# Sample's self-attention in units of a head and 256 queries, with background work dealt out per unit

## The chip, the cores and the metric

The kernel runs on one core of a Trainium2 chip. The metric is the device time of one execution, in microseconds (us). The engines are named as in the profile: PE is TensorE (matmuls; PEld are its weight loads), DVE is VectorE, ACT is ScalarE, POOL is GpSimd, SP is SyncE, which here issues every DMA, in order, from one queue.

## The reference

One layer of an encoder is applied to two groups of requests with the same weights: prompt (1024 tokens) and sample (512 tokens). Everything is in float32. What matters here:

```python
z = rms_norm(x, ln_pre) @ w_in          # q, k, v, gates, merge logits, pool and cross inputs
s = einsum('bqkgd,bskd->bkgqs', qblk, k) * HEAD_DIM ** -0.5   # 8 heads, 2 kv heads, head size 64
p = softmax(s)                          # over all 1024 (prompt) or 512 (sample) keys
attn_out = einsum('bkgqs,bskd->bqkgd', p, v)
cross_out = softmax(xq @ mk.T * XHD ** -0.5) @ mv             # 4 heads, 256 memory tokens
branches = pool_out * silu(g0), attn_out * silu(g1), cross_out * silu(g2)
merged = sum over n of sigmoid(merge_logits_n + b_n) * (branches[n] @ w_branch[n])
y = x + rms_norm(merged @ w_out, ln_post)
```

## The kernel before

Float32 products are made of float32r parts: a value is split in a high part (a copy on ACT) and a low part (a subtraction on DVE), `split` (L171), and a product takes three matmuls, or two where one side holds both parts side by side.

The projections of prompt come first, then those of sample that its attention needs. What is left of sample's projections (32 output tiles of 24 matmuls each: gates and merge logits) is the *fill*: `weave` (L108) emits it a half tile (12 matmuls) at a time between the steps of a *stream* of attention units, so that PE has work while the softmax of a unit runs on the other engines. When the stream is through, what is left of the fill is emitted, and then the branch projections of prompt (`branches(0, sc, merged)`, L1039), which load the prompt's branch outputs `br0`, `br2` and `br1` from DRAM.

The stream is (L1034 to L1037): prompt's self-attention (64 units), prompt's cross-attention (8), sample's self-attention (32), sample's cross-attention (4). A unit of self-attention is a head and 128 queries. It has four steps:

- `ahead`: the load of q, two units early.
- `scores`: matmuls of q with the keys into a PSUM tile `A` of 128x1024, the maximum (DVE), the exponential (ACT) with its sum read out, the reciprocal (DVE), the normalisation (POOL).
- `turn`, two units later: the transposes of the probabilities into a second `A` tile, and their split into `med` tiles.
- `values`, two more units later: the products with v into a PSUM tile `B`; then, for every pair of units, a copy of one half (L810, ACT), a sum (L811, DVE), and for every pair of heads the gating (L813, POOL) and the store to `br1` (L814).

There are two `A` buffers, and scores and transposes take them in turn, so the next unit's scores wait until the exponential of this unit has been read out. With 1024 keys a unit of prompt fills an `A` tile. With 512 keys a unit of sample fills half of it: two score matmuls, four transposes and four value matmuls, and a maximum, exponential, split on 512 columns.

`weave` adds up the PE cost of each step (a 512-column matmul counts 213 ns, a transpose 107 ns), times 0.66 (`SHARE`), and emits fill until that much is paid. A step that emits no matmuls earns no fill: in the first iterations of the stream there are scores alone.

The order on each engine is then decided by a scheduler, in which `high_priority` moves instructions ahead: the evacuations of PSUM by 200 (`EVAC`), the maximum and exponential by 150 (`PMAX`), the split of transposes by 150 (`PTURN`). The SP queue holds stores and loads in one order, and a store that waits for its data holds up the loads behind it.

## Time and profile before

| | |
|---|---|
| median of 3 runs | 1512.16 us (1507.26 to 1512.44) |
| profiled execution | 1511.38 us, span 1509.6 us |
| PE busy | 1462.9 us, 97% of the span |
| DVE, ACT, POOL busy | 981.2, 709.2, 272.4 us |
| the stream of attention units | from 695 to 1171.5 us of the span |
| sample's self-attention in it | from about 1047 to 1143 us |

PE is the engine that the span is made of; a microsecond is won or lost where PE stands still or runs at its lower clock. Rows of a timeline merge instructions of one kind that follow each other: start, length, engine, line, operation, tiles, and in brackets the time for which the engine sat idle before, with what ended it. A matmul's length holds its latency; what a matmul costs in a row of them is the distance of their starts.

### The profile page before, as it was taken

The numbers are of one execution on the slowest core, as the hardware profiler recorded it, in microseconds if no ns is written. First come the engines' busy times: TensorE is split into PE (matmuls) and PEld (weight loads), VectorE is DVE, ScalarE is ACT, GpSimd is POOL, SyncE is SP. The second block draws the span as 40 slices with busy tenths as digits, with TensorE's granted clock in tenths as the row PEclk, the third lists the DMA queues.
The fourth block names the chain that finished last, engine by engine and source line by source line (L and its number), as shares of the span: only waits on it lengthen the run. The fifth ranks groups of instructions, "written<-read, shape, count | busy, mean of one in ns | idle before, by whom it ended". The sixth has DMA issues, their size and how long they took to land.

```text
span 1509.6 us, 19658 instructions
## 1 busy us (share of the span) xinstructions
PE 1462.9 (97%) x7264; PEld 1207.9 (80%) x7264; DVE 981.2 (65%) x1262; ACT 709.2 (47%) x1097; POOL 272.4 (18%) x286
## 2 busy tenths in 40 slices
PE   5999999999999999999999999999989999999998
PEld 3778888888888888887888888888767878888887
DVE  5896586666648564646676676666667664764754
ACT  5354444544434544434565555666666323323332
POOL 0001020110000000301222222233233150150241
PEclk8999999999999999999999999999999999999999
DMA  7333234332323433344322222265326854954952
GB/s 274 100 112 110 84 112 126 106 132 65 127 91 93 155 119 126 112 138 138 91 65 78 96 65 90 81 213 185 126 72 233 313 179 138 338 192 141 337 163 84
DMA packets 88174, 211.37 MB, mean 140 GB/s; under 512 B 9872, under 2 KB 19216, under 8 KB 87312
## 3 DMA queue, kind: packets, MB, share of 16 engines
q1 hardware_dynamic: 88080, 210.14, 42.1%
q8 instruction: 57, 0.93, 0.3%
q14 instruction: 37, 0.30, 0.1%
HBM read 155.57 MB, written 54.53 MB: 139 GB/s over the span
## 4 chain that ended last, share of the span: by engine, by line
PE 83%; issue 4%; ACT 4%; DVE 4%; DMA 2%; POOL 1%; SPq 0%; DVEq 0%; POOLq 0%; ACTq 0%
PE B L133 65%; PE A L133 13%; PE A L137 5%; ACT u L769 1%; DMA hu<-xq 1%; DVE wlo L169 1%; ACT med L172 1%; ACT whi L172 1%; DVE s L767 1%; PE B L137 1%; DMA hu<-merge 1%; POOL med L925 1%; POOL s L196 0%; DVE med L169 0%; DMA med<-q 0%
## 5 line engine op out<-in xcount | busy, mean ns | idle before, releaser
L133 PE MATMUL B<-med,whi 128*128 128x512 f32 x2776 | 870.3, 393 | 1.1 <-ACT hu L359 1.1
L133 PEld LDWEIGHTS B<-med,whi 128*128 128x128 f32 x2776 | 513.5, 188 | 104.5 <-ACT hu L359 2.3
L133 PE MATMUL B<-med,wlo 128*128 128x512 f32 x1388 | 542.6, 391 | 0.7 <-DVE wlo L169 0.7
L172 ACT ACTIVATE whi<-raw 128x1024 fp32r<-128x1024 f32 (+1 forms) x168 | 167.3, 996 | 304.4 <-PE B L133 212.6
L133 PEld LDWEIGHTS B<-med,wlo 128*128 128x128 f32 x1388 | 260.7, 188 | 55.9 <-DVE wlo L169 1.7
L169 DVE TENSOR_TENSOR wlo<-raw,whi 128x1024 fp32r<-128x1024 f32 (+1 forms) x168 | 213.0, 1268 | 139.3 <-ACT whi L172 136.8
L172 ACT ACTIVATE med<-A 128x1024 fp32r<-128x1024 f32 (+1 forms) x108 | 96.9, 897 | 121.3 <-PE A L137 121.1
L771 POOL TENSOR_SCALAR u<-u,s 128x1024 f32<-128x1024 f32 (+1 forms) x96 | 94.6, 985 | 317.0 <-DVE s L770 275.7
L169 DVE TENSOR_TENSOR med<-A,med 128x1024 fp32r<-128x1024 f32 (+1 forms) x109 | 115.7, 1061 | 51.6 <-ACT med L172 50.0
L767 DVE TENSOR_REDUCE s<-A 128x1 f32<-128x1024 f32 (+1 forms) x96 | 100.1, 1043 | 42.7 <-PE A L133 20.8
L192 POOL TENSOR_SCALAR s<-s 128x16 f32<-128x16 f32 (+3 forms) x17 | 6.6, 388 | 671.8 <-DVE s L557 324.6
L769 ACT ACTIVATE u<-A,s 128x1024 f32<-128x1024 f32 (+1 forms) x96 | 93.1, 970 | 46.3 <-DVE s L767 45.8
L137 PE MATMUL A<-ident,u 128*128 128x128 f32 x784 | 107.2, 275 | 4.6 <-DVE med L169 2.1
L137 PEld LDWEIGHTS A<-ident,u 128*128 128x128 f32 x784 | 90.8, 141 | 24.8 <-issue 9.6
L133 PE MATMUL A<-kt,med 128*128 128x512 f32 x320 | 96.5, 415 | 10.0 <-ACT u L769 8.8
L925 POOL TENSOR_TENSOR med<-med,hu 128x512 f32<-128x512 f32 x48 | 77.4, 1625 | 136.1 <-DVE hu L923 136.1
L133 PE MATMUL A<-whi,med 128*128 128x512 f32 (+1 forms) x320 | 92.4, 368 | 0.2 <-ACT hu L954 0.2
L172 ACT ACTIVATE whi<-sum 128x1024 fp32r<-128x1024 f32 x50 | 53.1, 1062 | 64.3 <-PE B L133 62.1
L133 PEld LDWEIGHTS A<-kt,med 128*128 128x128 f32 x320 | 54.4, 190 | 34.2 <-ACT u L769 22.9
L133 PE MATMUL B<-med,vt 128*128 128x256 f32 x512 | 76.1, 288 | 1.4 <-ACT med L172 1.4
L169 DVE TENSOR_TENSOR med<-med,med 128x1024 fp32r<-128x1024 f32 (+1 forms) x50 | 55.5, 1115 | 33.7 <-ACT med L172 29.9
L172 ACT ACTIVATE med<-med 128x1024 fp32r<-128x1024 f32 (+1 forms) x44 | 44.3, 1019 | 68.8 <-POOL med L925 42.6
(173 smaller groups left out, 1567.2 us busy)
## 6 DMA issues: line engine op xcount, KB each, us to landing
raw<-wt SPq DMA_DIRECT2D x168, 512.0 KB, 3.7
merge<-hu SPq DMA_DIRECT2D x72, 256.0 KB, 2.1
hu<-merge SPq DMA_DIRECT2D x72, 256.0 KB, 5.4
med<-br SPq DMA_DIRECT2D x36, 256.0 KB, 5.2
q<-hu SPq DMA_DIRECT2D x24, 256.0 KB, 2.6
br<-hu SPq DMA_DIRECT2D x24, 256.0 KB, 2.5
med<-q SPq DMA_DIRECT2D x12, 512.0 KB, 4.5
med<-xt_prompt SPq DMA_DIRECT2D x4, 1024.0 KB, 13.2
```

The costliest lines, as they stand in the source:

```text
L133: pe.matmul(out, l, r, **k)
L137: pe.transpose(out, x, i[:])
L169: v.tensor_tensor(out, x, hi.bitcast(F32), op=ALU.subtract)
L172: act.activation(hi, x, AF.Copy)
L192: pool.tensor_scalar(ss, ss, EPS, 1.0, op0=ALU.add, op1=ALU.mult)
L767: v.reduce_max(mx[:], a[:, :L], axis=AX.X, negate=True)
L769: act.activation(p[:, :L], a[:, :L], AF.Exp, bias=mx[:], accum_out=sm[:])
L771: pool.tensor_scalar(p[:, :L], p[:, :L], rc[:], 1.0, op0=ALU.mult, op1=ALU.mult)
L925: pool.tensor_tensor(at, at, sg[:], op=ALU.add)
```

## The change

Sample's attention gets a function of its own, `pairs_of`, with units of a head and 256 queries (16 units). The two query tiles of a unit share one `A` tile: four score matmuls, one maximum over both, two exponentials (each with its own maximum and its own sum), one reciprocal, two normalisations, eight transposes into one `A` tile, one split of 1024 columns, eight value matmuls. The count of matmuls, transposes and exponentials of the whole kernel stays the same. The end of a unit (L803 to L814) moves into `gated`, which both kinds of attention call.

`weave` no longer measures a step's cost. Each unit carries a number (2560 for self-attention, 3410 for cross-attention), and each iteration of the stream yields a third of it, times `SHARE`, three times: after scores, turn and values, whether or not such a step exists in that iteration. So the first iterations earn as much fill as the later ones, and so do the last four, in which the units run out.

```diff
-    def weave(main, fill, share):
+    def weave(main, fill):
         owed = 0.0
-        for _ in with_cost(main):
-            owed += _ * share
+        for more in main:
+            owed += more
             while owed > 0:
                 c = cost[0]
                 if next(fill, fill) is fill:
...
+    def pairs_of(sc, kt, vt):
+        qd, gd, out = sc["q"], sc["attn_gate"], sc["br1"]
+        units = [(jp, hd) for jp in range(TT // 2) for hd in range(NH)]
...
+        def scores(i):
+            jp, hd = units[i]
+            g = hd // (NH // NG)
+            a, p = A(), U()
+            mx, sm, rc = S(2), S(2), S(2)
+            for j in range(2):
+                q, ns = state["q", jp][:, j * D + hd * P:j * D + (hd + 1) * P], slice(j * BLK, (j + 1) * BLK)
+                mm(a[:, ns], q, kt[g][0], start=True, stop=False)
+                mm(a[:, ns], q, kt[g][1], start=False, stop=True)
+            with tc.high_priority(PMAX):
+                v.reduce_max(mx[:], a[:].rearrange("p (j n) -> p j n", j=2), axis=AX.X, negate=True)
+                for j in range(2):
+                    ns = slice(j * BLK, (j + 1) * BLK)
+                    act.activation(p[:, ns], a[:, ns], AF.Exp, bias=mx[:, j:j + 1], accum_out=sm[:, j:j + 1])
+            v.reciprocal(rc[:], sm[:])
+            for j in range(2):
+                ns = slice(j * BLK, (j + 1) * BLK)
+                pool.tensor_scalar(p[:, ns], p[:, ns], rc[:, j:j + 1], 1.0, op0=ALU.mult, op1=ALU.mult)
+            state[i] = p
+
+        def turn(i):
+            p, tp, pt = state[i], A(), M()
+            for c in range(4):
+                for j in range(2):
+                    tr(tp[:, c * 256 + j * P:c * 256 + (j + 1) * P], p[:, j * BLK + c * P:j * BLK + (c + 1) * P], ident)
+            with tc.high_priority(PTURN):
+                split(pt[:, :D], pt[:, D:], tp[:])
+            state[i] = pt
...
+        return [(ahead, scores, turn, values, i, 2560) for i in range(len(units))]
...
     def stream(units):
         n = len(units)
         for i in range(-2, n + LAG + VLAG):
+            more = units[min(max(i, 0), n - 1)][5] * SHARE / 3
             for k, lag in enumerate((-2, 0, LAG, LAG + VLAG)):
                 if 0 <= i - lag < n:
                     units[i - lag][k](units[i - lag][4])
-                    yield
+                if k > 0 and i >= 0:
+                    yield more
...
-    units += attention(0, scs, kts, vts, 512) + cross(0, scs, mkd[0], mvd[0])
-    weave(stream(units), fill, SHARE)
+    units += pairs_of(scs, kts, vts) + cross(0, scs, mkd[0], mvd[0])
+    weave(stream(units), fill)
```

What this does to the order is shown at three places. In the rows after the change the line numbers are those of the changed kernel: L126 and L130 are the matmul and the transpose, L139 the load, L165 the copy of a split. The first is PE at the start of the stream, in the kernel before: the transposes of the first unit (`A<-ident` x8), three matmuls of a pool projection, the scores of the fourth unit (`A<-kt`), the transposes of the second unit, and the first value matmul (`B<-med,vt`).

```order
L137 MATMUL A_5482<-ident,u_5431 128x128 x8
L133 MATMUL B_5523<-med_5330,hu_5317 128x512 x3
L133 MATMUL A_5493<-kt_651,med_5419 128x512
L133 MATMUL A_5493<-kt_652,med_5419 128x512
L133 MATMUL A_5493<-kt_651,med_5419 128x512
L133 MATMUL A_5493<-kt_652,med_5419 128x512
L137 MATMUL A_5530<-ident,u_5463 128x128 x8
L133 MATMUL B_5567<-med_5480,vt_655 128x256
```

The same place on PE after the change (`B<-med,whi` and `B<-med,wlo` are fill):

```order
L130 MATMUL A_5506<-ident,u_5431 128x128 x8
L126 MATMUL B_5547<-med_4493,whi_5543 128x512 x2
L126 MATMUL B_5547<-med_4493,wlo_5544 128x512
L126 MATMUL B_5547<-med_4493,whi_5543 128x512 x2
L126 MATMUL B_5547<-med_4493,wlo_5544 128x512
L126 MATMUL B_5547<-med_4496,whi_5543 128x512 x2
L126 MATMUL B_5547<-med_4496,wlo_5544 128x512
L126 MATMUL B_5547<-med_4496,whi_5543 128x512 x2
L126 MATMUL B_5547<-med_4496,wlo_5544 128x512
L126 MATMUL A_5517<-kt_651,med_5419 128x512
```

Twelve matmuls of fill now stand between the first transposes and the fourth unit's scores, where three pool matmuls stood; those three, and two of fill, now stand between the second unit's transposes and the first value matmul.

The second place is ACT in the middle of sample's self-attention. Before, each unit has one split of its transposes (`med<-A`, L172) and one exponential (`u,s<-A`, L769); in between stand copies of value halves (L810), a tanh of the fill (L480) and the split of the fill's next weights (`whi<-raw`):

```order
L172 ACTIVATE med_9375<-A_9399 128x4x128
L769 ACTIVATE u_9395,s_9392<-A_9388,s_9391 128x512
L172 ACTIVATE med_9429<-A_9430 128x4x128
L480 ACTIVATE hu_9449<-B_9343,hbias 128x512
L769 ACTIVATE u_9425,s_9422<-A_9418,s_9421 128x512
L810 ACTIVATE hu_9410<-B_9452 64x256
L172 ACTIVATE whi_9721<-raw_9719 128x1024
L769 ACTIVATE u_9464,s_9461<-A_9457,s_9460 128x512
L172 ACTIVATE med_9429<-A_9468 128x4x128
```

After (L165 is the split, L825 the exponential, L860 the copy, L473 the tanh), three units in a row:

```order
L860 ACTIVATE hu_9322<-B_9354 64x256
L825 ACTIVATE u_9328,s_9330<-A_9327,s_9329 128x512 x2
L165 ACTIVATE med_9402<-A_9401 128x1024
L825 ACTIVATE u_9387,s_9389<-A_9386,s_9388 128x512
L860 ACTIVATE hu_9422<-B_9413 64x256
L825 ACTIVATE u_9387,s_9389<-A_9386,s_9388 128x512
L165 ACTIVATE med_9443<-A_9442 128x1024
L825 ACTIVATE u_9428,s_9430<-A_9427,s_9429 128x512
L473 ACTIVATE hu_9466<-B_9373,hbias 128x512
L860 ACTIVATE hu_9422<-B_9469 64x256
L825 ACTIVATE u_9428,s_9430<-A_9427,s_9429 128x512
L165 ACTIVATE whi_9680<-raw_9678 128x1024
```

The split now stands ahead of the unit's two exponentials, and in two units of three a copy, or a tanh and a copy, stands between the two. On PE the three units read: scores, 8 transposes, 5 value matmuls, 12 of fill; scores, 8 transposes, 8 value matmuls, 7 of fill; scores, 8 transposes, 5 of fill, 11 value matmuls.

The third place is the end of the stream, on PE and on SP. Before, on PE: the values of the last two heads of sample's cross-attention (`B<-med,med` x6 each), a last half tile of fill, and then the first branch matmul of prompt (`med_10328`, the split of `br0`):

```order
L133 MATMUL B_10286<-med_10230,med_9931 128x512 x6
L133 MATMUL B_10297<-med_10253,med_9931 128x512 x6
L133 MATMUL B_10273<-med_4499,whi_10269 128x512 x2
L133 MATMUL B_10273<-med_4499,wlo_10270 128x512
L133 MATMUL B_10273<-med_4499,whi_10269 128x512 x2
L133 MATMUL B_10273<-med_4499,wlo_10270 128x512
L133 MATMUL B_10273<-med_4502,whi_10269 128x512 x2
L133 MATMUL B_10273<-med_4502,wlo_10270 128x512
L133 MATMUL B_10273<-med_4502,whi_10269 128x512 x2
L133 MATMUL B_10273<-med_4502,wlo_10270 128x512
L133 MATMUL B_10344<-med_10328,whi_10338 128x512 x2
```

After, on PE (`med_10168` is the split of `br0`):

```order
L130 MATMUL A_10095<-ident,u_9973 128x128 x8
L126 MATMUL B_10107<-med_9992,med_9704 128x512 x6
L130 MATMUL A_10118<-ident,u_10026 128x128 x8
L126 MATMUL B_10130<-med_10064,med_9704 128x512 x6
L126 MATMUL B_10141<-med_10104,med_9704 128x512 x6
L126 MATMUL B_10152<-med_10127,med_9704 128x512 x6
L126 MATMUL B_10184<-med_10168,whi_10178 128x512
```

The fill is used up before the last two transposes, and the first branch matmul stands right behind the last value matmul. On SP before (`br_0_c` are the stores of sample's cross-attention heads, `med<-br_1_c` the four loads of prompt's `br0`):

```order
L814 DMA br_0_3_4512<-hu_10091 128x256
L885 DMA br_0_0_4513<-hu_10240 128x512
L146 DMA raw_10450<-wt 128x1024
L146 DMA med_10323<-br_1_0_595 128x512
L146 DMA med_10323<-br_1_1_596 128x512
L885 DMA br_0_1_4514<-hu_10263 128x512
L146 DMA med_10323<-br_1_2_597 128x512
L146 DMA med_10323<-br_1_3_598 128x512
L885 DMA br_0_2_4515<-hu_10293 128x512
L146 DMA u_11121<-x_prompt 128x1024
L885 DMA br_0_3_4516<-hu_10304 128x512
```

On SP after:

```order
L474 DMA merge_1_7_4544<-hu_10092 128x512
L139 DMA hu_10137<-x_gate_1_4522 128x512
L139 DMA hu_10148<-x_gate_2_4523 128x512
L139 DMA hu_10159<-x_gate_3_4524 128x512
L936 DMA br_0_0_4513<-hu_10114 128x512
L139 DMA med_10163<-br_1_0_595 128x512
L936 DMA br_0_1_4514<-hu_10137 128x512
L936 DMA br_0_2_4515<-hu_10148 128x512
L139 DMA med_10163<-br_1_1_596 128x512
L936 DMA br_0_3_4516<-hu_10159 128x512
L139 DMA med_10163<-br_1_2_597 128x512
L139 DMA med_10163<-br_1_3_598 128x512
```

The second load of `br0` now stands behind the third of the four stores, and the last two loads behind the fourth; before, all four stood ahead of the third.

## Rows read from the trace of the kernel before

**Rows 1.** Busy time by stretch: from:to, us, each engine, PE's clock, DMA.
```profile
704.00:716.00 12.00, 9.29 (x39) 7.44 (x40) 6.48 (x9) 4.64 (x8) 2.24 (x2) 0.72 0.34 99
...
750.00:1000.00 250.00, 246.74 (x1459) 207.53 (x1457) 167.65 (x207) 149.53 (x220) 67.21 (x64) 1.00 0.29 92
1047.00:1143.00 96.00, 88.84 (x498) 70.30 (x497) 65.68 (x122) 58.98 (x125) 29.43 (x40) 1.00 0.41 135
1143.00:1171.50 28.50, 27.46 (x162) 23.03 (x161) 19.92 (x27) 18.70 (x48) 9.32 (x18) 1.00 0.60 195
```

**Rows 2.** Timeline of PE at the start of the stream, fourth to sixth unit.
```profile
705.53 1.21 PE L133 MATMUL A<-kt,med 128*128 128x512 f32 x4 [1.84 <-ACT u L769]
...
706.81 1.84 PE L137 MATMUL A<-ident,u 128*128 128x128 f32 x8
...
709.76 0.58 PE L133 MATMUL B<-med,vt 128*128 128x256 f32 x1 [1.11 <-ACT med L172]
```

**Rows 3.** PE's groups from 1047 to 1143 us, shapes apart.
```profile
L133 PE MATMUL B<-med,whi 128*128 128x512 f32 x98 | 33.8, 403 | 0.0
L133 PE MATMUL A<-kt,med 128*128 128x512 f32 x64 | 22.2, 428 | 5.1 <-ACT u L769 5.0
L133 PE MATMUL B<-med,med 128*128 128x256 f32 x116 | 20.3, 293 | 0.2 <-ACT med L172 0.2
L137 PE MATMUL A<-ident,u 128*128 128x128 f32 x136 | 20.2, 273 | 1.8 <-DVE med L169 1.5 <-ACT u L769 0.2
L133 PE MATMUL B<-med,wlo 128*128 128x512 f32 x48 | 19.1, 397 | 0.0
L133 PE MATMUL B<-med,med 128*128 128x512 f32 x24 | 6.4, 402 | 0.0
L133 PE MATMUL A<-med,u 128*128 128x256 f32 x12 | 1.7, 292 | 0.0
```

**Rows 4.** Timeline of one prompt unit, from scores to the next scores.
```profile
764.70 1.08 PE L133 MATMUL A<-kt,med 128*128 128x512 f32 x4
...
765.61 1.03 PE L137 MATMUL A<-ident,u 128*128 128x128 f32 x8
...
766.40 1.19 PE L133 MATMUL B<-med,vt 128*128 128x256 f32 x8
766.68 1.02 ACT L172 ACTIVATE med<-A 128x1024 fp32r<-128x1024 f32 x1 [2.35 <-PE A L137]
767.43 0.64 PE L133 MATMUL B<-med,whi 128*128 128x512 f32 x2
767.60 1.11 ACT L769 ACTIVATE u<-A,s 128x1024 f32<-128x1024 f32 x1
...
768.83 0.38 ACT L810 ACTIVATE hu<-B 64x256 f32<-64x256 f32 x1
768.86 1.19 PE L133 MATMUL A<-kt,med 128*128 128x512 f32 x4
```

**Rows 5.** Timeline of ACT in sample's self-attention.
```profile
1074.90 0.68 ACT L769 ACTIVATE u<-A,s 128x512 f32<-128x512 f32 x1
...
1075.56 0.69 ACT L480 ACTIVATE hu<-B,hbias 128x512 f32<-128x512 f32 x1
1076.13 1.06 ACT L172 ACTIVATE whi<-raw 128x1024 fp32r<-128x1024 f32 x1
```

**Rows 6.** Timeline of the stream's end.
```profile
1166.05 2.88 PE L133 MATMUL B<-med,med 128*128 128x512 f32 x12
1166.20 0.93 SPq L146 DMA_DIRECT2D med<-br  x2
...
1167.61 0.69 DVE L884 TENSOR_TENSOR hu<-B,hu 128x512 f32<-128x512 f32 x1 [0.67 <-PE B L133]
...
1170.54 1.06 ACT L172 ACTIVATE med<-med 128x1024 fp32r<-128x1024 f32 x1 [3.07 <-DMA med<-br]
...
1171.63 1.23 DVE L169 TENSOR_TENSOR med<-med,med 128x1024 fp32r<-128x1024 f32 x1 [1.59 <-ACT med L172]
```

72 lines of the change are left out of this document (41 added, 31 removed).

## The prediction

> **What bounds the kernel now.** I read the page's busy shares first: PE works 97% of the span, so what counts is where PE stands still, runs at its lower clock, or is made to wait by what the change moves. Then I read the stretches of the stream [rows 1]. While prompt's self-attention runs in its steady state (750 to 1000 us) PE is idle 250 - 246.74 = 3.3 us, 1.3%. In sample's self-attention (1047 to 1143) it is idle 96 - 88.84 = 7.2 us, 7.5%. At the end of the stream (1143 to 1171.5) it is idle 1.0 us. The stretch from 704 to 716 is odd: 2.7 us idle, and a granted clock of 0.72, where the other stretches have 1.00. The timeline there [rows 2] shows PE waiting 1.84 us for an exponential, then running eight transposes in 1.84 us that take 1.03 us elsewhere [rows 4], which is the 1.2 GHz level, and then waiting 1.11 us for a split.
>
> Busy time flatters PE, since a matmul's length holds its latency. So I also count work by the distance of starts. Twelve 512-column matmuls last 2.88 us together [rows 6], one by itself 0.40 [rows 3]: (2.88 - 0.40) / 11 = 0.225 each. Eight transposes take 766.40 - 765.61 = 0.79, eight value matmuls 767.43 - 766.40 = 1.03, four score matmuls 765.61 - 764.70 = 0.91 [rows 4]. From 1047 to 1143 there are 98 + 48 + 64 + 24 = 234 matmuls of 512 columns (52.7 us), 116 + 12 of 256 (16.5) and 136 transposes (13.4) [rows 3]: 82.6 us of work in 96, so 13.4 us are lost there, not 7.2.
>
> The sum below is made against the profiled execution, 1511.38 us, which lies 0.8 us under the median of the runs.
>
> **Start of the stream.** The change deals fill to iterations in which no transposes or values exist yet. By the order, the first wait (1.84) gets 12 fill matmuls in front of it instead of 3 pool matmuls: 9 x 0.225 = 2.0 us more cover, enough. The second (1.11) gets five matmuls, 1.13 us, in front of it, where there was nothing. Both waits go: 2.9 us. The clock goes with them. A mean of 0.72 over 12 us is (1 - 0.72) x 12 / 0.5 = 6.7 us at half rate; 1.1 of it was the second wait, and the rest did 2.8 us of work in 5.6. Together 5.7 us; I take 5.5 as the gain. The bounds are 0, if the waits only move to the next unit, and 5.7. The matmuls used here are not extra; they are taken from the end of the stream, which is the third term.
>
> **Sample's self-attention.** Work on PE is the same: a unit of four scores, eight transposes, eight values and on average eight of fill is 0.91 + 0.79 + 1.03 + 1.80 = 4.53 us. What can hold it is the `A` buffer: the next scores wait for this unit's exponentials. In the prompt unit [rows 4] that chain is: scores at 764.70, transposes at 765.61, their split on ACT at 766.68, the exponential behind it at 767.60, next scores at 768.86, together 4.16. After the change the split still goes first on ACT, by the order, and instead of one exponential on 1024 columns there are two on 512, each with its own sum read. From the start of the exponential to the next scores the prompt unit takes 1.26, of which 1.11 is the exponential; with two of 0.68 [rows 5] it is 0.68 + 0.68 + 0.15 = 1.51. So the chain is 4.16 - 1.26 + 1.51 = 4.41. In two units of three a copy of value halves stands between the two exponentials (0.38, [rows 4]): 4.79. In one of these a tanh as well, whose place costs 1076.13 - 1075.56 = 0.57 [rows 5]: 5.36.
>
> Against this stands what PE has to do until the next scores. Scores, transposes, 5 values, 12 of fill: 0.91 + 0.79 + 0.64 + 2.70 = 5.04, no wait. Scores, transposes, 8 values, 7 of fill: 4.31, wait 0.48. Scores, transposes, 5 of fill, 11 values: 0.91 + 0.79 + 1.13 + 1.42 = 4.25, wait 1.11. That is 1.6 us lost per three units. The first four units have the six wider matmuls of the cross-attention in place of values and little to wait for; the other twelve make four rounds, 6.4 us, and I add 0.7 for the small losses that the prompt stretch has too. So 7 of the 13.4 us stay lost, and the gain is 6. Bounds: 0, where ACT's chain is as long as the pairs take now, and 12, if the stretch came down to the 1.3% of the prompt stretch. I take 6, since the chain is made of rows. DVE loses sixteen maxima and sixteen low-part subtractions as instructions of their own; it is not in the chain, as the maximum runs beside transposes and split, so I cost this at nothing; without that cover each of the sixteen units could pay a subtraction more, 1.23 us [rows 6].
>
> **End of the stream.** Here the change costs. Before, the last half tile of fill (12 x 0.225 = 2.7 us) stands between the last values and the first branch matmul, and the four loads of `br0` stand ahead of the third cross-attention store. After, the fill is used up two heads earlier, and the second load of `br0` is queued on SP behind the third store, the last two behind the fourth. A store waits for DVE's gating of its head (0.69, [rows 6]), that for the head's values. Let E be the end of the last values. The third head's values end 6 x 0.225 = 1.35 before E, its gating some 0.5 before E, the second load is issued at about E. In the trace a pair of these loads is issued at 1166.20 and the split that waits for it starts at 1170.54, 4.3 us later [rows 6]. So the split runs from E + 4.3 to E + 5.4 (1.06, [rows 6]); two branch matmuls can run on the high part, 0.45, and the low part is there at E + 6.6 (1.23). PE loses 5.4 + 0.8 = 6.2. The loads behind the fourth store go out at about E + 1.3 and are split by E + 6.7, just behind. What now stands in front of the gate loads `x_gate`, the store of the last pair of heads of the self-attention, may hold DVE's gating by another 0 to 2 us; I take 0.3, so 6.5. The bounds are 3.5 (if a single load lands in 2 us less) and 8.5. Of this the 1.0 us of idle time before [rows 1] is to be taken off: a loss of 5.5.
>
> A PE that stands for 6 us is three times the wait that preceded the 1.2 GHz stretch in [rows 2], and here it is one piece. I expect the same stretch of 6.7 us behind it, and as PE has work all through it, it costs half, 3.4 us. The Trainium skill says in "TensorE: Matmul & The Clock Gate", section "HAM oscillation — how this bites in real kernels", that a wait for a transfer can send the clock down, so that the next work starts at the lower level. The trace agrees with it at 706.81 [rows 2], where transposes ran at half rate behind a wait; it speaks against it from 1047 to 1143, where 7.2 us of idle time in pieces left the clock at 1.00 [rows 1]. By that rule the sum has these 3.4 us, without it it has not; the case without is a rival below.
>
> **Sum.** 1511.4 - 5.5 - 6 + 5.5 + 3.4 = 1508.8. The cross-attention units of sample get other fill between them; from [rows 1] all their stretch has 1.0 us to win and I count nothing. Forecast 1508.5 us. A measurement of this kernel can tell some 0.5% from no change, 7.6 us about the median: faster is below 1504.6, slower above 1519.7. The forecast is no change that can be told.
>
> **The rivals.**
> - *The gap at the end without the lower clock.* For it: the 1.00 of sample's stretch. Against it: that gap is in one piece. Then 1508.5 - 3.4 = 1505, on the edge; half of its chance falls under 1504.6.
> - *No gap at the end.* The loads of `br0` come early enough, because DVE and SP run ahead of what I counted or the transfer is short. For it: before, the same kind of wait cost PE nothing, though ACT waited 3.07 us for the loads [rows 6]. Against it: then 12 fill matmuls covered it, now none stand there. The end costs as before, and 1511.4 - 11.5 = 1500: faster.
> - *The change does not do at the start what it says.* PE meets the same wait, at the next unit, and the clock falls as before. For it: ACT also has the fill's weight split and a copy there. Against it: the order puts nothing between that PE would run out of. 1508.5 + 5.5 = 1514.
> - *ACT becomes the bound of sample's units.* If the fill's weight split (1.06, [rows 5]) comes between the transposes' split and the exponentials, a unit takes 4.79 + 1.06 = 5.85 us against a bare 4.53: 16 x 1.32 = 21 us lost where 13.4 are lost now, 7.7 more in place of 6 less. With the other terms that is 1508.5 + 13.7 = 1522. Without sample's term the sum is 1514.8, so it makes the kernel slower by 0.5% once these units lose (13.4 + 4.9) / 16 = 1.14 us each, from a unit of 5.7 us on. For it: two sum reads and up to two evacuations already stand in the chain. Against it: the order has the weight split ahead of the transposes' split, in time that ACT spends waiting.
>
> **How the numbers follow.** Forecast 0.45; no lower clock at the end 0.17; no gap 0.20; start unchanged 0.08; ACT the bound 0.10. Faster is 0.20, half of 0.17, and 0.03 of the forecast's own spread: 0.31. Slower is 0.10. No change is the rest, 0.59. The range has to hold the forecast with its neighbours on both sides, 1500 and 1514, and leaves out the slow case and the outer half of the fast one: 1499 to 1516. The forecast's own range, from the bounds of the end (2 to 3 either way) and of sample's waits (3), is 1504 to 1513.
>
> **What would show it.** In the profile after: no idle time of PE over 0.5 us in the first 20 us of the stream and a clock of 1.00 there; sample's units 4.9 to 5.2 us apart, with PE's waits on the exponential (the two of a unit, with copy and tanh between) and none on DVE; a gap of PE of about 6 us before the first branch matmul, ended by the split of `br0`, with the loads issued behind the stores of the cross-attention; and behind the gap a clock of 0.5 for some 7 us. The prediction is wrong if the gap is under 3 us, if the start still waits, or if the units of sample stand over 5.6 us apart.

## The result, and the profile after

| | before | after |
|---|---|---|
| median (lowest to highest), 4 runs each | 1509.88 us (1507.26 to 1512.44) | 1498.22 us (1496.52 to 1501.38) |
| profiled execution, span | 1511.38, 1509.6 | 1497.91, 1496.1 |

The ratio is 0.9924, 95% interval 0.9903 to 0.9944: 0.8% faster by the medians (11.7 us; 13.5 between the two profiled executions), where 1508.5 us and "no change that can be told" were forecast. The median lies 0.8 us under the lower end of the range. The stretches after, with the columns of [rows 1]:

```profile
704.00:716.00 12.00, 12.00 (x68) 9.72 (x67) 9.49 (x13) 7.06 (x11) 3.36 (x3) 1.00 0.30 105
750.00:1000.00 250.00, 247.54 (x1470) 208.78 (x1469) 167.93 (x208) 150.16 (x223) 68.24 (x65) 1.00 0.30 99
1041.00:1120.00 79.00, 78.19 (x450) 65.86 (x448) 56.86 (x71) 51.89 (x103) 25.72 (x38) 1.00 0.46 149
1151.50:1164.00 12.50, 6.92 (x17) 4.93 (x18) 4.12 (x5) 2.11 (x2) 0.00 (x0) 0.73 1.00 339
```

Against [rows 1]: the start has no idle time left and a clock of 1.00 for 0.72; sample's self-attention is idle for 0.8 us of 79, where it was 7.2 of 96; behind it stands a new stretch with 5.6 us of idle time and a clock of 0.73.

The start on PE, which answers to [rows 2]. The transposes of the second unit follow the scores without a wait and last 1.04 us, where they lasted 1.84:

```profile
705.68 1.18 PE L126 MATMUL A<-kt,med 128*128 128x512 f32 x4
706.71 1.04 PE L130 MATMUL A<-ident,u 128*128 128x128 f32 x8
707.50 0.94 PE L126 MATMUL B<-med,hu 128*128 128x512 f32 x3
```

A unit in the middle of sample, on PE: scores, transposes, and 4.37 us later the next scores, directly behind fill.

```profile
1081.49 1.09 PE L126 MATMUL A<-kt,med 128*128 128x512 f32 x4
1082.42 1.04 PE L130 MATMUL A<-ident,u 128*128 128x128 f32 x8
1085.64 0.39 PE L126 MATMUL B<-med,whi 128*128 128x512 f32 x1
1085.86 1.16 PE L126 MATMUL A<-kt,med 128*128 128x512 f32 x4
```

The same time on ACT (L165 the split of the transposes, L825 the two exponentials with their sum reads, L860 the copy of value halves):

```profile
1083.49 1.02 ACT L165 ACTIVATE med<-A 128x1024 fp32r<-128x1024 f32 x1 [2.25 <-PE A L130]
1084.41 0.68 ACT L825 ACTIVATE u<-A,s 128x512 f32<-128x512 f32 x1
1085.21 0.38 ACT L860 ACTIVATE hu<-B 64x256 f32<-64x256 f32 x1
1085.61 0.69 ACT L825 ACTIVATE u<-A,s 128x512 f32<-128x512 f32 x1
1086.20 0.19 ACT L825 ACTIVATION_READ_ACCUMULATOR u<-A,s 128x1 f32 x1
```

And on DVE, the low part of the same split:

```profile
1084.55 1.23 DVE L162 TENSOR_TENSOR med<-A,med 128x1024 fp32r<-128x1024 f32 x1 [0.65 <-ACT med L165]
```

ACT runs in the order that was forecast: split, exponential, copy, exponential, the last one done at 1085.61 + 0.69 = 1086.30, 4.81 us behind the scores. (The forecast has 4.79 for this kind of unit, up to the next scores, so 4.64 to the end of the exponential.) But the next scores start at 1085.86, when the second exponential is still reading its `A` tile. They can't be writing that tile, so they write the other one, which the low part of the split gave free at 1084.55 + 1.23 = 1085.78. The exponential's tile is left to the transposes, which start one row of scores later, at 1086.86, when it is free too. The prediction had the scores wait for the exponential.

This is not one unit alone. By the semaphores in the trace, what the scores waited for last was the low part of a split in 8 of sample's 16 units, and it ended 0.04 to 0.08 us before they started. In the five units in which it was an exponential of sample's own, that had ended at least 0.24 us before. The units stand 4.94 us apart on average. PE's waits from 1041 to 1112 say the same (what waited, for whom: us in total, times, longest). Before, scores (L133) waited for the exponential:

```profile
PE A L133 <- ACT u L769: 3.3, 3, 1.6
```

After, there is no such row; the scores' weight loads (PEld, which overlap with matmuls) wait for the low part:

```profile
PEld A L126 <- DVE med L162: 1.2, 5, 0.3
```

The end of the stream on PE: the last values, the gap, and the first branch matmul, which answers to [rows 6]. The last two rows are pairs of branch matmuls, the first at the lower clock, the second behind it.

```profile
1146.89 4.37 PE L126 MATMUL B<-med,med 128*128 128x512 f32 x18
1157.03 2.05 PE L126 MATMUL B<-med,whi 128*128 128x512 f32 x3 [5.78 <-ACT med L165]
1159.31 1.05 PE L126 MATMUL B<-med,whi 128*128 128x512 f32 x2
1164.42 0.61 PE L126 MATMUL B<-med,whi 128*128 128x512 f32 x2
```

SP's queue at that time (length is the time to issue):

```profile
1148.52 0.32 SPq L936 DMA_DIRECT2D br<-hu  x1
1148.88 0.43 SPq L139 DMA_DIRECT2D med<-br  x1
1151.21 1.00 SPq L936 DMA_DIRECT2D br<-hu  x2
1152.26 0.45 SPq L139 DMA_DIRECT2D med<-br  x1
1152.80 0.40 SPq L936 DMA_DIRECT2D br<-hu  x1
1153.25 0.94 SPq L139 DMA_DIRECT2D med<-br  x2
```

DVE's gating, for which the stores wait, and which itself waits for a gate load:

```profile
1150.49 2.12 DVE L935 TENSOR_TENSOR hu<-B,hu 128x512 f32<-128x512 f32 x3 [0.87 <-DMA hu<-x_gate]
```

The first load of `br0` (`med<-br`) goes out behind the first store, the second only at 1152.26, behind the third, the last two behind the fourth. This is the order that the forecast's third term had, and the gap is 5.78 us (forecast 5.4 to the first matmul).

**Where the time went.** For the table I cut the trace at six matmuls: the first scores, the 13th unit's scores, sample's first and last scores, the last values of the stream, and the first matmul of the output projection. From each piece I take off what its matmuls need by the prediction's distances (0.225 us for 512 columns, 0.79 / 8 for a transpose, here 0.127 for 256 columns). What is left is lost time; the table gives it for before, and for every other kernel its difference to before, in us. Since the transposes and values of sample's last units come behind its last scores, they are in the piece of sample's cross-attention. The piece ahead of the stream is left out: there the same instructions differ by up to 2.6 us between executions. Each row is one execution, so small differences in it can be chance.

```
                      start  prompt  sample  sample's  gap and   output   sum
                             + cross self    cross     branches  projection
before, lost           10.1    16.6    13.4     3.2      0.5       4.3
after                  -6.8    -1.7    -9.8    -1.7     +9.2      -2.0    -12.8
pairs only             -0.1    +0.2    -9.4    -0.2     +0.3       0.0     -9.2
even fill only         -6.8    -1.0    -0.8    -0.4    +10.4      -1.8     -0.4
buffers in turn        -6.5    -0.5    -3.8    +1.4     +2.6      +0.6     -6.2
two maxima             -6.8    -1.6    -6.7    -2.2    +10.1      -2.0     -9.2
two splits             -6.8    -1.6    -8.3    +2.7     +1.5      +0.4    -12.1
two of each            -6.8    -1.6    -8.3    +0.6     +2.2      +0.1    -13.8
SHARE 0.60             -6.2    +6.2    -9.6    -1.9      0.0      -1.9    -13.4
fill by stage          -6.8    -0.7    -7.3    -0.9     +0.1      +0.5    -15.1
loads early            -6.8    -1.6    -9.8    -1.9     +6.0      -0.6    -14.7
gap filled             -6.8    -1.5    -9.8    -2.2     +6.8      -1.0    -14.5
loads, fill 2800       -6.9    -0.8    -8.7    +0.3     +1.2      -0.8    -15.7
loads, fill 2600       -6.9    -1.7    -9.8    -2.3      0.0      -0.3    -21.0
```

(In "gap filled", the 20 added matmuls, 4.5 us, count as lost.)

### The profile page after: what moved, and what is told of

Same layout as the page of the kernel before. It is cut to its first block, busy times and chain, and to the rows that moved or that the text cites. A ratio compares the mean times of both kernels' runs of the same rounds, so it can differ in the third digit from the quotient of the medians.

```text
span 1496.1 us, 19562 instructions
## 1 busy us (share of the span) xinstructions
PE 1456.9 (97%) x7264; PEld 1211.1 (81%) x7264; DVE 976.8 (65%) x1214; ACT 708.3 (47%) x1081; POOL 272.2 (18%) x286
## 4 chain that ended last, share of the span: by engine, by line
PE 86%; ACT 4%; issue 4%; DVE 3%; DMA 2%; POOL 1%; SPq 0%; DVEq 0%; POOLq 0%; ACTq 0%
PE B L126 67%; PE A L126 13%; PE A L130 5%; ACT u L762 1%; DVE s L760 1%; ACT whi L165 1%; PE B L130 1%; ACT med L165 1%; DVE wlo L162 1%; DMA hu<-xq 0%; POOL s L189 0%; DMA u<-x_prompt 0%; DVE u L998 0%; DMA med<-q 0%; DMA hu<-wt 0%
## 5 line engine op out<-in xcount | busy, mean ns | idle before, releaser
L126 PE MATMUL B<-med,whi 128*128 128x512 f32 x2776 | 868.5, 393 | 6.9 <-ACT med L165 5.8
L126 PEld LDWEIGHTS B<-med,whi 128*128 128x128 f32 x2776 | 514.4, 188 | 112.0 <-ACT med L165 6.4
L126 PE MATMUL B<-med,wlo 128*128 128x512 f32 x1388 | 543.1, 391 | 0.5 <-DVE wlo L162 0.5
L165 ACT ACTIVATE whi<-raw 128x1024 fp32r<-128x1024 f32 (+1 forms) x168 | 167.4, 996 | 302.4 <-PE B L126 206.4
L126 PEld LDWEIGHTS B<-med,wlo 128*128 128x128 f32 x1388 | 261.3, 188 | 56.3 <-DVE wlo L162 1.3
L165 ACT ACTIVATE med<-A 128x1024 fp32r<-128x1024 f32 x92 | 94.3, 1025 | 109.1 <-PE A L130 108.9
L764 POOL TENSOR_SCALAR u<-u,s 128x1024 f32<-128x1024 f32 x64 | 72.4, 1131 | 251.7 <-DVE s L763 219.4
L130 PE MATMUL A<-ident,u 128*128 128x128 f32 x784 | 102.8, 273 | 0.9
L130 PEld LDWEIGHTS A<-ident,u 128*128 128x128 f32 x784 | 90.1, 140 | 16.2 <-issue 5.1
L760 DVE TENSOR_REDUCE s<-A 128x1 f32<-128x1024 f32 x64 | 78.1, 1220 | 33.0 <-PE A L126 11.5
L126 PE MATMUL A<-kt,med 128*128 128x512 f32 x320 | 92.0, 409 | 2.9 <-ACT u L762 1.2
L126 PE MATMUL A<-whi,med 128*128 128x512 f32 (+1 forms) x320 | 92.4, 368 | 0.2 <-ACT hu L1005 0.2
L762 ACT ACTIVATE u<-A,s 128x1024 f32<-128x1024 f32 x64 | 71.2, 1113 | 38.6 <-DVE s L760 38.2
L165 ACT ACTIVATE whi<-sum 128x1024 fp32r<-128x1024 f32 x50 | 53.1, 1062 | 64.2 <-PE B L126 63.1
L165 ACT ACTIVATE med<-med 128x1024 fp32r<-128x1024 f32 (+1 forms) x44 | 44.3, 1018 | 71.8 <-POOL med L976 36.8
L126 PE MATMUL B<-med,vt 128*128 128x256 f32 x512 | 76.0, 287 | 0.4 <-ACT med L165 0.4
L162 DVE TENSOR_TENSOR wlo<-sum,whi 128x1024 fp32r<-128x1024 f32 x50 | 61.1, 1222 | 23.1 <-ACT whi L165 22.2
```

The costliest lines, as they stand in the source:

```text
L126: pe.matmul(out, l, r, **k)
L130: pe.transpose(out, x, i[:])
L162: v.tensor_tensor(out, x, hi.bitcast(F32), op=ALU.subtract)
L165: act.activation(hi, x, AF.Copy)
L760: v.reduce_max(mx[:], a[:], axis=AX.X, negate=True)
L762: act.activation(p, a[:], AF.Exp, bias=mx[:], accum_out=sm[:])
```

## The experiments

The question after the result: the sum missed by 11 us, and the gap had come as forecast, so more must have been won elsewhere. My theory was the buffer seen above; the rivals were that the even dealing filled sample's units, or that one maximum and one split were worth more than I had counted. Then: what the gap and the lower clock cost, and whether they can be had back. In the expectations, "the changed kernel" is the one after.

### One part at a time

*Pairs only*: the changed kernel with the old `weave`.

```diff
-    weave(stream(units), fill)
+    weave(stream(units), fill, SHARE)    # with_cost, and a yield per step, as before
```

> Only the pairs (16 units of 256 queries), with the old dealing of fill by measured cost. Theory A (the whole gain in sample comes from the pairs, because the next scores take whichever of the two A buffers is free): the start of the stream is as in the kernel before (two waits of 1.84 and 1.11 us, clock 0.72 in 704:716), sample's units about 4.9 us apart with under 2 us of idle time over the 16 units, 12 fill matmuls left behind the last values and so no gap of PE over 1 us there: 12 to 13 us faster than the kernel before, 1497 to 1499 us. Rival B (the even dealing is what filled sample's units; the pairs alone leave the forecast's 7 us lost): 6 us faster, about 1504 us. Rival C (without even dealing there is also a gap at the end, as two of the four loads of br0 stand behind the second and third store of the cross-attention): 5 us slower than A says, 1503 us, and then PE shows the gap.

Measured: 1501.18 us, ratio 0.9933 (0.9915 to 0.9952).

```profile
704.00:716.00 12.00, 10.84 (x50) 8.70 (x49) 5.51 (x9) 4.24 (x6) 3.35 (x3) 0.72 0.23 83
1041.00:1120.00 79.00, 78.42 (x447) 65.75 (x446) 53.72 (x69) 52.18 (x108) 26.60 (x38) 1.00 0.44 140
```

The start is as in [rows 1], clock 0.72; sample is idle for 0.6 us of 79. So sample's gain is the pairs' (-9.4 alone, -9.8 with even fill) and rival B is out. There is no gap (+0.3 in the table), so C is out too. The total is 2 us above A's range, as A had counted 12 to 13 us for sample; that the pairs make sample's gain is borne out, its size is not.

*Even fill only*: the changed kernel with `attention(0, scs, kts, vts, 512)`, 32 units of half the fill, for `pairs_of`.

```diff
-    units += pairs_of(scs, kts, vts) + cross(0, scs, mkd[0], mvd[0])
+    units += attention(0, scs, kts, vts, 512) + cross(0, scs, mkd[0], mvd[0])
```

> Only the even dealing of fill, with the 32 units of 128 queries in sample's attention as before. Theory A: the start of the stream is won (5.5 to 6 us, clock 1.00 in 704:716), sample's 32 units lose some 13 us as in the kernel before (their scores wait for the exponential, 0.5 us each), and the end has the gap of about 6 us and 6 to 7 us at half clock behind it (9 us lost): 3 us slower than the kernel before, 1511 to 1514 us. Rival B (the even dealing itself fills sample's units): sample loses under 5 us, 5 us faster, about 1504 us.

Measured: 1511.37 us, ratio 1.0000 (0.9990 to 1.0011). In A's range, though A had counted 3 us lost against the kernel before, and none are. Sample's stretch, and the first branch matmul:

```profile
1041.00:1120.00 79.00, 73.88 (x408) 57.45 (x407) 55.68 (x104) 48.00 (x104) 23.50 (x36) 1.00 0.35 110
```

```profile
1169.08 2.05 PE L126 MATMUL B<-med,whi 128*128 128x512 f32 x3 [6.94 <-ACT med L165]
```

Sample is idle for 5.1 us, the gap is 6.94 us. Even dealing by itself wins some 10 us at the start, in prompt and in the output projection and gives them back at the end. The two halves of the change do not quite add up: -9.2 and -0.4 against -12.8. Of the 3.2 us between them, 1.5 are in the gap and branches, 1.1 in sample's cross-attention and 0.9 in prompt.

### Which buffer the scores take

*Buffers in turn*: sample's scores always in one `A` tile, its transposes in the other; elsewhere the two alternate.

```diff
-            a, p = A(), U()                      # scores of pairs_of
+            a, p = A(k=0), U()
-            p, tp, pt = state[i], A(), M()       # turn of pairs_of
+            p, tp, pt = state[i], A(k=1), M()
```

> The changed kernel, but with the two A buffers under two names: sample's scores always take the first and its transposes always the second; elsewhere they alternate. So the next scores can only start behind both exponentials of this unit, which is what the prediction had assumed. Theory A (the forecast's chain is right, it only didn't apply, as the scores took the buffer that the transposes' split had freed): PE shows waits of scores on the exponential of 0.5 to 1.1 us in two units of three, 5 to 8 us lost over the 16 units, 1503 to 1506 us. Rival B (the chain was counted too long; ACT has room, so the buffer doesn't matter): within 2 us of the changed kernel, 1498 to 1500 us, and no waits of scores on the exponential over 0.3 us.

Measured: 1504.50 us, ratio 0.9953 (0.9935 to 0.9971): A's range. In sample 5.9 us are lost against the changed kernel, where A had 5 to 8. That the total lies in the range too is partly chance: with the buffers in turn everywhere, 1.2 us more are lost in prompt, 3.1 in sample's cross-attention and 2.6 in the output projection, and the gap is 6.6 smaller. PE's waits from 1041 to 1112 (L130 is the matmul here, L134 the transpose, L829 the exponential, L833 the normalisation):

```profile
PEld A L134 <- POOL u L833: 4.9, 13, 0.5
PEld A L130 <- ACT u L829: 2.5, 8, 0.4
```

The size in sample is near the 6.4 us that the prediction counted for the wait, the place only in part: the scores wait for the exponential (2.5 us), but more is lost one step on, where the transposes wait for POOL's normalisation.

*Two maxima*, *two splits*, *two of each*: these undo "one maximum and one split for both" and keep the common tile.

```diff
-                v.reduce_max(mx[:], a[:].rearrange("p (j n) -> p j n", j=2), axis=AX.X, negate=True)
+                for j in range(2):
+                    ns = slice(j * BLK, (j + 1) * BLK)
+                    v.reduce_max(mx[:, j:j + 1], a[:, ns], axis=AX.X, negate=True)
...
-                split(pt[:, :D], pt[:, D:], tp[:])
+                for j in range(2):
+                    ns = slice(j * BLK, (j + 1) * BLK)
+                    split(pt[:, ns], pt[:, D:][:, ns], tp[:, ns])
```

> The changed kernel with two maxima of 512 columns in each of sample's units instead of one of 1024; the split stays one. By its own duration this costs DVE 2 x 0.687 - 1.225 = 0.15 us a unit, 2.4 us over the 16, beside other work. By the order, though, 13 of the 16 units' scores now wait for the exponential of the unit before, where 9 in the changed kernel wait for the low part of the transposes' split alone. Theory A (what the pairs win hangs on which buffer the next scores take): 4 to 7 us lost in sample, as with the buffers in turn, 1502 to 1505 us, with waits of scores on the exponential. Rival B (only the durations count): under 2 us lost, 1498 to 1500 us.

Measured: 1502.33 us, ratio 0.9940 (0.9923 to 0.9956). The total is in A's range; the loss in sample against the changed kernel, 3.0 us, lies between A's 4 to 7 and B's 2. From 1041 to 1112, scores wait for the exponential 4.7 us in weight loads and 0.8 in matmuls, where the changed kernel has no such row:

```profile
PEld A L126 <- ACT u L825: 4.7, 10, 0.8
PE A L126 <- ACT u L825: 0.8, 2, 0.4
```

Sample then loses 6.7 us in all (13.4 - 6.7). That is close to the prediction's 7, but 3.7 of it are lost in the changed kernel too, without this wait, so the wait costs 3.0 where 6.4 were counted. DVE's own extra 2.4 us lie beside it and aren't told apart.

> The changed kernel with the split of the transposes in two halves of 512 columns on ACT and on DVE; the maximum stays one. By the durations: ACT 2 x 0.596 - 1.03 = 0.16 us, DVE 2 x 0.691 - 1.221 = 0.16 us a unit. By the order 8 units' scores wait for the exponential alone and 7 for DVE and ACT. Theory A (the buffer): 2 to 5 us lost in sample, between the changed kernel and the one with two maxima, 1500 to 1503 us. Rival B (only the durations count): under 3 us, 1498 to 1500 us. Rival C (one split for both is what the pairs win): most of the 11 us that the pairs won are lost, 1507 us.

Measured: 1498.85 us, ratio 0.9917 (0.9901 to 0.9934). Sample loses 1.5 us more than in the changed kernel. The total lies in B's range by offsets: the last units and the loads of `br0` come to stand otherwise, so that 4.4 us more are lost in sample's cross-attention and 2.4 in the output projection, and the gap is 7.7 us smaller.

> The changed kernel with two maxima and two splits in each of sample's units: of the pairing only the common buffer and the common step are left. By the order 14 of 16 units' scores wait for the exponential. Theory A (the buffer, and a chain longer by 0.16 on ACT): 6 to 9 us lost in sample, 1504 to 1507 us. Rival B (only the durations count, 0.3 us a unit on either engine): 2 to 4 us, 1500 to 1502 us. Rival C (one maximum and one split are all that the pairs win): 11 us lost, 1509 us.

Measured: 1497.38 us, ratio 0.9908 (0.9891 to 0.9924). Below every theory's figure; here too the gap is smaller, by 7.0 us, and 2.3 more are lost in sample's cross-attention. In sample 1.5 us more are lost than in the changed kernel, though in most units the scores wait for the exponential:

```profile
PEld A L126 <- ACT u L825: 3.2, 7, 0.6
PE A L126 <- ACT u L825: 0.4, 2, 0.2
```

So C is out: in sample's self-attention one maximum and one split are worth at most 1.5 of the 9.8 us, and by the totals nothing that can be told (1498.85 and 1497.38 us against 1498.22). The other 8.3 come with the common tile and step of 256 queries, which were not taken apart further. And A is only partly borne out. Making the scores wait for the exponential costs 5.9, 3.0 and 1.5 us in three forms. That the buffer matters is shown; why the wait is shorter in the last form is not.

### The end: gap, clock, and where the fill goes

*SHARE 0.60*:

```diff
-LAG, VLAG, SHARE, LOOK, WAIT = 2, 2, 0.66, 1, 6
+LAG, VLAG, SHARE, LOOK, WAIT = 2, 2, 0.60, 1, 6
```

> The changed kernel with SHARE 0.60 for 0.66: each unit earns 9% less fill (some 0.7 matmuls, 0.15 us), and 36 matmuls of fill (36 x 0.225 = 8.1 us) are left behind the last values, where the changed kernel has none. Theory A (the gap at the end costs 5.8 us and the lower clock behind it 3.3, and units of prompt have 0.2 us to spare in their chain, so that the fill taken from them costs nothing): no gap of PE over 1 us before the first branch matmul, clock 1.00 there, 9 us faster than the changed kernel, 1488 to 1490 us. Rival B (the units need the fill: each of some 90 units then waits 0.1 to 0.15 us longer): 9 won, 9 to 13 lost, 1498 to 1502 us, and the idle time of PE in 750:1000 grows from 2.5 to over 6 us. Rival C (only the gap goes, and the clock falls elsewhere): 1492 us.

Measured: 1498.17 us, ratio 0.9916 (0.9898 to 0.9934): B. No gap, and 9.2 us won there; but prompt pays:

```profile
750.00:1000.00 250.00, 243.93 (x1454) 204.81 (x1453) 171.19 (x210) 150.82 (x227) 70.51 (x69) 1.00 0.30 98
```

6.1 us idle for 2.5, over all of prompt 7.9 us. Sample, with 9% less fill, loses nothing (-9.6). So fill may be taken there:

*Fill by stage*: 2100 for 2560 in `pairs_of`, 2800 for 3410 in `cross`, which makes prompt's eight cross-attention units too.

```diff
-        return [(ahead, scores, turn, values, i, 2560) for i in range(len(units))]    # pairs_of
+        return [(ahead, scores, turn, values, i, 2100) for i in range(len(units))]
-        return [(ahead, scores, turn, values, c, 3410) for c in range(NXH)]           # cross
+        return [(ahead, scores, turn, values, c, 2800) for c in range(NXH)]
```

> The changed kernel with the fill taken from other units than in the run with SHARE 0.60: prompt's units earn as before (2560), sample's pairs earn 2100 for 2560 and the cross-attentions 2800 for 3410, so that 24 matmuls of fill (5.4 us) are left behind the last values, and the loads of br0 stand one store earlier on SP. Theory A (prompt's units have no time to spare, sample's pairs and the cross-attentions have): the stretch 750:1000 keeps its 2.5 us of idle time, sample's units come closer to each other (4.5 us for 4.9), the gap at the end and the lower clock behind it go: 9 us faster than the changed kernel, 1488 to 1490 us. Rival B (sample's pairs need their fill as prompt's units do, 0.3 us each): 5 us of the 9 are lost again, 1493 to 1495 us. Rival C (as with SHARE 0.60, nothing is won): 1498 us.

Measured: 1494.93 us, ratio 0.9892 (0.9876 to 0.9908): B. The gap is gone, sample loses 2.5 us more with 18% less fill, 2.5 us are lost in the output projection, and 1.0 in the piece of prompt, whose cross-attention also earns less.

*Loads early*: the loads of `br0` ahead of the first store.

```diff
-        t = from_scratch(field, bs)
+        with tc.high_priority(BRANCH):        # 300
+            t = from_scratch(field, bs)
```

> The changed kernel, with the four loads of br0 issued on SP ahead of the first store of sample's cross-attention; PE's order is the same, no fill is kept. Theory A (the gap of 5.8 us is made by the place of the loads in SP's queue, behind stores that wait for DVE): the split of br0 is done before the last values end, no gap over 1 us, clock 1.00 behind it, 9 us faster than the changed kernel, 1488 to 1490 us. Rival B (the loads now wait for a buffer and hold up the stores behind them, or their split waits for ACT and DVE): a gap of 2 to 4 us is left and with it the lower clock, 1494 to 1497 us. Rival C (the place in the queue was not it): 1498 us.

Measured: 1495.89 us, ratio 0.9894 (0.9875 to 0.9912): B. PE, SP and ACT at the end:

```profile
1155.42 0.97 PE L126 MATMUL B<-med,whi 128*128 128x512 f32 x3 [3.75 <-ACT med L165]
```

```profile
1147.29 1.87 SPq L139 DMA_DIRECT2D med<-br  x4
```

```profile
1154.31 1.06 ACT L165 ACTIVATE med<-med 128x1024 fp32r<-128x1024 f32 x1 [5.70 <-DMA med<-br]
```

Counted from the start of the last values (1147.30 here, 1146.89 in the changed kernel) the first load goes out 2.0 us earlier and the other three 4.9 to 5.4, but the split, which needs the first two, starts only 2.0 us earlier. The loads take longer. How long they take to land, in the changed kernel (1145 to 1158) and then here (1143 to 1156; KB of each, median us):

```profile
med<-br SPq DMA_DIRECT2D x4, 256.0 KB, 4.0
```

```profile
med<-br SPq DMA_DIRECT2D x4, 256.0 KB, 6.5
```

So the place in the queue was part of the gap, but only 2 us of it; most of what the earlier issue gave, the transfers took back.

*Gap filled*: 20 matmuls that nothing reads, between the last values and the branches.

```diff
     run(fill)
+    idle = B()
+    for _ in range(20):
+        mm(idle[:], identr[:], hs[0][0], start=_ == 0, stop=_ == 19)
     run(branches(0, sc, merged))
```

> The changed kernel, with 20 matmuls of 512 columns (4.5 us) behind the last values that nothing reads; the loads of br0 and all else stay where they are. It adds work and removes none. Theory A (the clock fell because PE stood still in one piece; the fall costs 3.3 us by itself): the first branch matmul starts at the same distance from the last values as before (6.1 us), the clock stays at 1.00 behind it, 3.3 us faster than the changed kernel, 1494 to 1496 us. Rival B (the fall has another cause, or the 20 matmuls only delay the branch matmuls): 1498 us or slower, and 0.5 in the records behind the gap.

Measured: 1494.97 us, ratio 0.9892 (0.9876 to 0.9907): A.

```profile
1145.32 4.37 PE L126 MATMUL B<-med,med 128*128 128x512 f32 x18
1149.53 4.75 PE L126 MATMUL B<-med,identr 128*128 128x512 f32 x20
1155.76 1.75 PE L126 MATMUL B<-med,whi 128*128 128x512 f32 x5 [1.48 <-ACT med L165]
```

```profile
1150.00:1165.00 15.00, 13.45 (x58) 10.47 (x57) 6.57 (x8) 3.18 (x3) 0.00 (x0) 1.00 0.95 329
```

The first branch matmul stands as far from the start of the last values as before (1155.76 - 1145.32 = 10.4; 1157.03 - 1146.89 = 10.1), the clock stays at 1.00, and from there to the first matmul of the output projection (1221.63, and 1225.62 in the changed kernel) it takes 65.9 us for 68.6. So the lower clock cost some 2.7 us; the medians are 3.3 us apart.

*Loads and fill*, with 2800 and with 2600 in `cross`, 2560 in the pairs, and the early loads. These two put the findings together.

> The changed kernel with the loads of br0 ahead of the first store of the cross-attention, and 2800 for 3410 as the fill that a cross-attention unit earns: by the order 24 matmuls of fill then stand between the last eighteen value matmuls of the stream, none behind them, and the loads stand ahead of two of the gate loads too. Sample's pairs earn as in the changed kernel. Theory A (the gap is the time from the loads' issue to the end of their splits, 4.3 to 6.5 us and 2.3, less what PE still has to do then; 24 x 0.225 + 18 x 0.225 = 9.4 us stand there): no gap over 1 us, clock 1.00, sample as in the changed kernel: 1488 to 1490 us; 1490 to 1492 if the out-projection's first weights come late, as they did in the run in which fill was kept from the pairs. Rival B (the cross-attentions need the fill that is taken from them): 3 us lost there, 1492 to 1494 us.

Measured: 1493.65 us, ratio 0.9886 (0.9868 to 0.9904): B. The gap is gone, but the losses are in many places, the largest in sample's cross-attention (2.0 us against the changed kernel), where transposes wait for POOL's four normalisations:

```profile
1144.42 1.22 PE L130 MATMUL A<-ident,u 128*128 128x128 f32 x6 [1.11 <-POOL u L913]
```

```profile
1141.64 3.17 POOL L913 TENSOR_SCALAR u<-u,s 128x256 f32<-128x256 f32 x4 [0.17 <-DVE s L910]
```

> As the run with 2800, with 2600: 12 matmuls of fill (2.7 us) are left behind the last values, as in the kernel before. Theory A: no gap, clock 1.00, 1488 to 1490 us, or 2 us more if the first weights of the out-projection come late, as they did in both kernels so far that left 12 or 24 matmuls. Rival B (the cross-attentions need the fill): 4 us lost in them, 1493 to 1495 us.

Measured: **1487.13 us** (1486.72 to 1488.73), ratio 0.9843 (0.9825 to 0.9861), faster than both kernels: 1.6% under the one before, and 0.9 us under A's range.

```profile
1140.00:1165.00 25.00, 25.00 (x112) 20.72 (x111) 13.40 (x15) 7.21 (x8) 0.00 (x0) 1.00 0.95 339
```

```profile
1138.12 1.85 SPq L139 DMA_DIRECT2D med<-br  x4
```

```profile
1144.53 1.06 ACT L165 ACTIVATE med<-med 128x1024 fp32r<-128x1024 f32 x1 [3.21 <-DMA med<-br]
```

The loads go out from 1138.12 on, the split starts 6.4 us later, 2.1 us before the last values end (1146.66), and PE never stands. Sample's cross-attention has less fill and loses less than in the changed kernel (-2.3 against -1.7). That 2600 does better than 2800 was not expected; the two differ in how the last units fall, and why that matters is open.

## Why the prediction was wrong

By its own terms, from the table (us; minus is faster):

| step | forecast | measured | |
|---|---|---|---|
| start of the stream, with its clock | -5.5 | -6.8 | right; a little more beyond 716 us |
| prompt after the start | not counted | -1.7 | missed |
| sample's self-attention | -6 | -9.8 | **failed** |
| sample's cross-attention | 0 | -1.7 | missed |
| gap at the end and lower clock | +5.5, +3.4 | +9.2 together | right, each part off by 0.7 to 1.0 |
| output projection | not counted | -2.0 | missed |
| sum | -2.6 | -12.8 | |

The rest to the measured 13.5 lies ahead of the stream and behind the last matmul. Sample (3.8 us) and the three zeros (5.4) make 9.2 of the 10.9 us by which the sum of 1508.8 missed the profiled execution; either alone would have left it in the range, at 1505.0 or 1503.4.

**The step that failed** is "the next scores wait for this unit's exponentials", and with it "7 of the 13.4 us stay lost". The chain on ACT came out 0.2 us longer in the unit shown, and PE's content was right: a unit of eight values and seven of fill took 4.37 us where 4.31 was forecast. But the one did not hold up the other. The prediction took it, as the text on the kernel before says, that scores and transposes use the `A` tiles in turn. In the units looked at here the scores took the tile that was free first, and that was not always the same one. In the prompt unit of [rows 4], from which the chain was read, the exponential ended at 767.60 + 1.11 = 768.71 and the low part of the split only at 767.74 + 1.23 = 768.97, behind the next scores at 768.86. They can only have taken the exponential's tile:

```profile
767.74 1.23 DVE L169 TENSOR_TENSOR med<-A,med 128x1024 fp32r<-128x1024 f32 x1 [0.65 <-ACT med L172]
```

With two exponentials and a copy the order turns round: in the unit shown after the change the low part was done 4.29 us behind the scores, the exponential 4.81. The trace before could have told it: 768.97 - 764.70 = 4.27 us from the scores to the end of the low part, against the forecast's 4.41, 4.79 and 5.36. The sign that the prediction named, waits on the exponential and none on DVE, came out the other way round; its spacing of 4.9 to 5.2 us did not tell the two apart.

As it ran, 3.7 us stayed lost (13.44 - 9.76, before rounding). With the wait put back it was 9.6 (buffers in turn) and 6.7 (two maxima), 5.9 and 3.0 more, where the prediction had counted 6.4 for it; two splits gave 5.2 and two of each 5.1. So the wait was priced high as well, a little against the first form and twofold or more against the others. The bound of 12 had contained what was measured.

**Three zeros made more than that step**: -1.7, -1.7 and -2.0. The one for sample's cross-attention rests on busy time, of which the prediction itself says that it flatters PE: there was 1.0 us of idle time to win, but 3.2 us were lost by the distances. Prompt behind its start and the output projection do not stand in the sum at all. For prompt, even dealing gives iterations the same fill; "even fill only" has -1.0 there, "pairs only" no gain. What makes prompt's other 0.7 isn't shown. The cross-attention gains only with both parts together (-0.2 and -0.4 alone), and why is open too. In the output projection PE waited for low parts of weights, in the kernel before from 1236 to 1248:

```profile
PE A L133 <- DVE wlo L169: 1.0, 2, 0.9
```

```profile
PEld A L133 <- DVE wlo L169: 1.9, 2, 1.3
```

After the change no such wait is there. It comes and goes with kernels whose end differs (gone in "even fill only", "two maxima" and "SHARE 0.60", there in "pairs only", "fill by stage" and "two splits"), so not with the gap alone; what decides it is open.

**The start held, and the end held in its steps, with sizes that made up for each other.** At the start, no idle time and clock 1.00. At the end: forecast, split at E + 4.3 and first matmul at E + 5.4; measured, with E = 1146.89 + 4.37 = 1151.26, 1155.93 = E + 4.7 and 1157.03 = E + 5.8. The second load went out 1.0 us later than forecast (1152.26), and the split started 3.7 us behind it instead of 4.3. The clock was 0.73 over 12.5 us, (1 - 0.73) x 12.5 / 0.5 = 6.75 us at half rate (forecast 6.7); it cost 2.7 us by the kernel with the gap filled, forecast 3.4. So of the 9.2 us some 6.5 are the wait (forecast 5.5): the sum was closer than its two parts. The rule cited from the Trainium skill, "TensorE: Matmul & The Clock Gate", section "HAM oscillation — how this bites in real kernels", held here: the wait for a transfer was followed by 1.2 GHz, and with all but 1.48 us of the wait filled, in that kernel, it was not.

**The rivals.** "No gap at the end" had the nearest number, 1500, by a way that did not happen: the gap came with all its price. The total agrees with that rival only because sample and the three zeros won 9 us more.

## What to carry to other kernels

Before a wait on a buffer is charged, see which buffer the instruction really takes: with two buffers and a scheduler it may be the one that another step frees, and that can change when the units change size. Fill that is spread evenly must be weighed at the place it is taken from: here prompt, whose units had no slack, paid 7.9 us for 9% less, sample nothing for 9% and 2.5 us for 18%, and the last transfer of a stage needs its own cover. When a large gain and a large loss are both forecast, check the stretches set to zero, since their sum can decide.

## What was not expected of the hardware

- The lower clock after a wait is not in proportion to it. A gap of 5.78 us was followed by 6.75 us at 1.2 GHz. With the loads early it was 3.75 us, and (1 - 0.89) x 15 / 0.5 = 3.3 us (the row below). With the gap filled it was 1.48 us, and none. At the start of the stream before, waits of 1.84 and 1.11 us came with 6.7 us [rows 1, 2], while in sample's self-attention before, single waits of up to 1.6 us left the clock at 1.00.

```profile
1150.00:1165.00 15.00, 10.96 (x41) 8.33 (x40) 6.59 (x9) 3.17 (x3) 0.00 (x0) 0.89 0.94 313
```

- The four loads of `br0` (256 KB each) landed 4.0 us behind their issue (median) in the changed kernel, where stores stood between them. Issued back to back they took 6.5 us ("loads early") and 5.9 (the fastest kernel), but 3.9 in the kernel with 2800 (the row below, from 1140 to 1150). So the spacing of the issues does not explain it by itself. Nor does the busy share of the DMA engines: between issue and split it was 0.96 to 0.99 in the changed kernel and 0.84 to 0.92 with the loads early. What does was not tried. One difference is what SP had issued just ahead: three gate loads in the 2 us before with the loads early, one with 2800.

```profile
med<-br SPq DMA_DIRECT2D x4, 256.0 KB, 3.9
```
